# The MLP of a two-layer decoder in four parts of 16 up tiles, the up tiles of a part between the down pairs of the part before

## The chip, the core and the metric

The kernel runs on one core of a Trainium2 chip. A core has a matrix engine (TensorE, PE in the profile; its weight loads are a row of their own, PEld), a vector engine (VectorE, DVE), a scalar engine (ScalarE, ACT), GpSimd (POOL, unused here) and SyncE (SP), which here only issues DMAs. Each engine works through its own list of instructions in order and waits on semaphores. The metric is the device time of one execution in microseconds (us), lower is better.

## The reference, cut to what matters

A decoder of two layers on 256 positions of width 2048: retention, then an MLP and a gated embedding, then block attention, a second MLP and a second gated embedding. The change touches the two MLPs:

```python
def rms_norm(x, g):
    y = xf * lax.rsqrt(jnp.mean(xf * xf, axis=-1, keepdims=True) + RMS_EPS)
    return y * g
def sq_relu_mlp(xn, w_up, w_down):
    return jnp.square(jax.nn.relu(xn @ w_up)) @ w_down
...
h = h + sq_relu_mlp(rms_norm(h, mlp_norm_g[i]), mlp_w_up[i], mlp_w_down[i])
```

`w_up` is 2048 x 8192, `w_down` 8192 x 2048, all in float32.

## The kernel before

**Operands.** TensorE is fed float32r operands, and float32 accuracy is rebuilt from two of them. Each weight unit (128 x 1024 of raw float32 from a DMA) is split: ACT casts it to a high part `wh` (L254), DVE subtracts that from the raw value and leaves the low part `wl` (L255). Activations are split in the same way. A product is then three matmuls: high by high, high by low, low by high. All weights go through one stream: a ring of three raw buffers of 1 MB (`raw`, a DMA each on SP), a ring of three pairs `wh`/`wl` (`RING`), and a list `prep` of splits with a due time, counted in matmul units. `run` walks over the units: it records the splits that are due, then the unit's matmuls, then what hangs on that unit (`at`). So the order on ACT and DVE is that of due times, and how far they run ahead of PE is set by the rings.

**Up.** An up tile is 128 of the 8192 columns, kept transposed: two weight units, 32 matmuls, with the weights as the stationary operand (`phase_a`, `mm_a`, L186 and L188), into one bank of PSUM. `evac_up` takes it out: ACT copies the first half (L259), DVE adds the second (`fold`, L260), DVE squares the positive part in one instruction (L756), and `block` splits it into `a` (L609, L611).

**Down.** A pair is 256 of the 8192 rows by 1024 columns, 1 MB of weights; a `sweep` runs over pairs and adds into four banks C00, C01, C10 and C11 (two halves of positions by two of columns); `g` is the half of the 2048 output columns. An ordinary pair needs eight products of 2 x 2 blocks, three matmuls each: 24. A fast pair (`FAST`) uses a Winograd form with seven products, 21 matmuls: `sums` forms three sums of weight blocks on DVE (L731 to L733, tile `tsum`), `corner` splits the three blocks that are used as they are (1536 columns), `wide` splits the sums (2048 columns), and on the activation side `combine` forms four sums `sf` and splits them into `sh` and `sl`. Four shared banks (P1, P5, Q6, Q7) go into the results at the end of a sweep (`shared`), beside the four C banks (`collect`, L685).

**Order.** The MLP runs in two halves: 32 up tiles, then two sweeps (g = 0 and 1) of 16 pairs, of which 3, 5, 7, 9, 11 and 13 are fast; then the same again. So a layer has four sweeps with six fast pairs each.

PSUM has eight banks: four for tiles and C banks (`mm`), two `y`, two `aux`.

Of the kernel before, what the change touches and what calls it, by code (L numbers as in the profile page):

```python
# [24 lines left out]
RV = RH * RDV  # L25
AH, DH = 16, 128
GH = 4
FF = 4 * D
FH = FF // 2
PD = 256  # L30
RMS_EPS = 1e-6
GN_EPS = 1e-5
# [53 lines left out]
class Core:  # L86
# [10 lines left out]
        self.slots.append(s)  # L97
        return s

    def unit(self, src, j, mm):  # L100
# [25 lines left out]
    def narrow(self, s, u):  # L126
# [3 lines left out]
        self.split(s["h"][:, u], s["l"][:, u], raw[:, u])  # L130
        self.spent += u

    def wide(self, s, src, n):
        self.operand(s)
        h, l = (s[x].rearrange("p a b -> p (a b)")[:, :n] for x in "hl")
        self.split(h, l, src.rearrange("p a b -> p (a b)")[:, :n])

    def run(self):
        for fn in self.tasks.pop(-1, []):
# [47 lines left out]
                else:  # L187
                    mm(ps, wh[:, c], rhs[k], start=first and k == 0, stop=end)  # L188

    def phase_a(self, name, src, base, tiles, per, lead, rhs, evac):  # L190

        banks = {}
        for j, (n, u) in enumerate(order_a(tiles, per, lead)):
            def mm(wh, wl, n=n, u=u):
                if u == 0:
                    banks[n] = self.bank(f"{name}{n}", *(("y", 2) if 4 <= n < lead else ()))
                self.mm_a(banks[n], wh, wl, [rhs(u * 8 + k) for k in range(8)], u == 0, u == per - 1, u % 2 == 1)
            i = self.unit(src, base + j, mm)
# [258 lines left out]
    def retention(self):  # L457
        nc = self.nc
        mm = nc.tensor.matmul
        x, ot = {}, {}  # L460
        first = len(self.units)
# [8 lines left out]
        for hd in range(RH):  # L470
            b, st = len(self.units), {}
# [93 lines left out]
                self.at(b + 25 + c, lambda c=c, q=2 * hd + c, i=b + 25 + c, turn=turn: self.steps(i, turn(q, 2 * c)))  # L565

        for g in range(2):
            self.sweep(f"ret_out{g}_", "ret_out", g * RV // 256, RET_ORDER, RET_FAST, x, g, ((1, 2), (3, 4)) if g else ((3, 4), (5, 6)), G_MLP0)

    def add(self, gains):  # L570
        def evac(c, banks, i):
# [56 lines left out]
            x[q, name] = h[:, n * P:(n + 1) * P], l[:, n * P:(n + 1) * P]  # L628
        yield

    def sweep(self, name, src, first, order, fast, x, g, when, gain, rows=None):

        banks, left = {}, {}
        tags = {"P1": "y", "P5": "y", "Q6": "aux", "Q7": "aux"}

        def add(s, ops):
            for bank, _, _ in ops:
                left[bank] = left.get(bank, 0) + 1

            def mm():  # L640
                h, l = (s[n].rearrange("p a (b c) -> p (a b) c", b=2) for n in "hl")
                m = self.nc.tensor.matmul
                for bank, which, j in ops:
                    start = bank not in banks
                    if start:
                        banks[bank] = self.bank(f"{name}{bank}_", *((tags[bank], 2) if bank in tags else ()))
                    left[bank] -= 1
                    ps, (xh, xl) = banks[bank], x[which]
                    m(ps, xh, h[:, j], start=start, stop=False)
                    m(ps, xh, l[:, j], start=False, stop=False)  # L650
                    m(ps, xl, h[:, j], start=False, stop=left[bank] == 0)
# [83 lines left out]
    def mlp(self, layer, gains):  # L735
        nc = self.nc
        v = nc.vector
        st = {}
        b = len(self.units)

        def rows():
            st["r2"] = self.cp.tile([P, 4], F32, name="r2", tag="r2", bufs=2)
            v.tensor_mul(st["r2"][:, :2], self.rn, self.rn)
            v.tensor_scalar_mul(st["r2"][:, 2:], st["r2"][:, :2], -1.0)
        self.at(b + 4, self.stats_a)
        self.at(b + 6, rows)
        x, pair = {}, {}
        for half in range(2):
            def evac_up(n, ps, half=half):
                q = n // 2  # L750
                if n % 2 == 0:
                    pair[q] = self.slot("t", (P, 2, S))
                t = pair[q][:, n % 2]
                self.fold(t, ps)
                yield
                v.scalar_tensor_tensor(t, t, 0.0, t, op0=ALU.max, op1=ALU.mult)  # L756
                parts = []
                if n % 2:
                    z = pair.pop(q)
                    if q in FAST:  # L760
                        parts.append(self.combine(x, q, z.rearrange("p a b -> p (a b)")))
                        next(parts[0])
                yield
                yield from self.both([self.block(x, st, n, t, q in FAST and n % 2 == 0)] + parts)
            self.phase_a(f"up{half}_", f"mlp_up{layer}", half * 64, 32, 2, 1 if half else UPLEAD, lambda k: self.xx[k], evac_up)
# [361 lines left out]
```

## Time and profile before

| | |
|---|---|
| median of 3 runs | 2720.79 us (2720.36 to 2720.8) |
| the profiled execution: its own time | 2720.18 us |
| its span | 2718.4 us |
| DVE busy | 1986.8 us (73%), 2603 instructions |
| ACT busy | 1365.0 us (50%), 1790 instructions |
| PEld busy | 2300.2 us (85%) |
| read from HBM | 517.39 MB, 191 GB/s over the span |

The span goes from the first to the last instruction of the profiled execution; its own time is 1.8 us longer. A start in the timeline is us from the start of the span. A row of the timeline has the start, the duration, the engine, the line, the operation with output and inputs, and in brackets the idle time of the engine ahead of it and what ended that. The matmuls are pipelined: one shows a duration of 0.39 us, but the next starts much earlier, so that PE's progress is read from the distance of starts.

In layer 0 the MLP runs from about 740 to 1430 us, with the first sweeps from 917 and again from 1261 us; in layer 1 the same comes about 1178 us later.

### The profile page before, as it was taken

What the parts mean: (1) busy time and instruction counts of PE and PEld (TensorE: products, weight loads), DVE (VectorE), ACT (ScalarE), POOL (GpSimd) and SP (SyncE); (2) the same over time, 40 slices, a digit from 0 to 9 for tenths busy, and PEclk for the clock granted to TensorE, in tenths of its full rate; (3) what the DMA queues carried; (4) which work ended last, traced back from release to release, by engine and by line L of the source; (5) the groups of instructions that cost most, each with busy time, mean ns of one, the idle gap of its engine ahead of it and who ended that gap; (6) DMA issues with size and microseconds to landing.
All of it is one profiled execution on the core that took longest, in us unless ns stands there. A gap on an engine that the chain in (4) does not pass through costs nothing.

```text
span 2718.4 us, 33914 instructions
## 1 busy us (share of the span) xinstructions
PE 2705.2 (100%) x13564; PEld 2300.2 (85%) x13564; DVE 1986.8 (73%) x2603; ACT 1365.0 (50%) x1790; POOL 0.2 (0%) x4
## 2 busy tenths in 40 slices
PE   9999999999999999999999999999999999999998
PEld 8888888888888888888888888888888888888886
DVE  7766666678876688666896777775666887668875
ACT  6444444445544445444556555555444544445564
POOL 0000000000000000000000000000000000000000
PEclk9999999999999999999999999999999999999999
DMA  7555455545565556555564555555554655555553
GB/s 287 189 189 188 176 187 189 176 171 198 213 201 188 179 208 217 186 186 186 200 218 174 193 180 178 177 186 178 193 188 174 222 187 207 186 177 209 194 215 139
DMA packets 79449, 522.47 MB, mean 192 GB/s; under 512 B 8987, under 2 KB 12988, under 8 KB 17596
## 3 DMA queue, kind: packets, MB, share of 16 engines
q1 hardware_dynamic: 78476, 519.20, 53.3%
q8 instruction: 106, 1.74, 0.2%
q10 hardware_dynamic: 816, 1.11, 0.2%
q14 instruction: 51, 0.42, 0.0%
HBM read 517.39 MB, written 2.88 MB: 191 GB/s over the span
## 4 chain that ended last, share of the span: by engine, by line
PE 97%; DVE 2%; ACT 1%; issue 0%; DVEq 0%
PE up L188 17%; PE up L186 9%; PE qk L188 4%; PE ak L188 2%; PE qk L186 2%; PE aq L188 2%; PE ak L186 1%; PE aq L186 1%; DVE wl L255 1%; PE xt L294 1%; PE y L526 1%; PE qk L215 1%; PE pu L797 0%; DVE h L685 0%; ACT wh L254 0%
## 5 line engine op out<-in xcount | busy, mean ns | idle before, releaser
L255 DVE TENSOR_TENSOR wl<-raw,wh 128x1024 fp32r<-128x1024 f32 (+3 forms) x811 | 1113.4, 1389 | 336.9 <-ACT wh L254 335.8
L254 ACT CAST wh<-raw 128x1024 fp32r<-128x1024 f32 (+3 forms) x811 | 935.4, 1185 | 305.6 <-issue 49.6
L188 PE MATMUL up<-x,wh 128*128 128x512 f32 x2048 | 491.5, 391 | 0.0
L188 PEld LDWEIGHTS up<-x,wh 128*128 128x128 f32 x2048 | 375.7, 188 | 72.3
L186 PEld LDWEIGHTS up<-x,wl 128*128 128x128 f32 x2048 | 263.9, 191 | 11.4 <-DVE wl L255 0.6
L186 PE MATMUL up<-x,wl 128*128 128x256 f32 x2048 | 267.5, 283 | 0.0
L259 ACT COPY t<-up 128x256 f32<-128x256 f32 x128 | 47.6, 372 | 365.2 <-PE up L188 365.2
L254 ACT CAST wh<-tsum 128x2048 fp32r<-128x2048 f32 x60 | 114.8, 1914 | 197.9 <-DVE tsum L733 189.9
L255 DVE TENSOR_TENSOR wl<-tsum,wh 128x2048 fp32r<-128x2048 f32 x60 | 137.6, 2293 | 24.4 <-ACT wh L254 24.4
L260 DVE TENSOR_TENSOR t<-t,up 128x256 f32<-128x256 f32 x128 | 53.9, 421 | 115.4 <-ACT t L259 115.4
L188 PE MATMUL qk<-x,wh 128*128 128x512 f32 x448 | 110.0, 392 | 0.0
L188 PEld LDWEIGHTS qk<-x,wh 128*128 128x128 f32 x448 | 81.8, 188 | 15.6
L731 DVE TENSOR_TENSOR tsum<-raw 128x1024 f32<-128x1024 f32 x60 | 73.1, 1219 | 0.0
L188 PE MATMUL aq<-x,wh 128*128 128x512 f32 x256 | 63.2, 391 | 0.0
L188 PE MATMUL ak<-x,wh 128*128 128x512 f32 x256 | 62.9, 391 | 0.0
L186 PE MATMUL qk<-x,wl 128*128 128x256 f32 x448 | 59.8, 284 | 0.0
L186 PEld LDWEIGHTS qk<-x,wl 128*128 128x128 f32 x448 | 57.8, 191 | 2.2
L287 ACT ACTIVATE sq<-h 128x512 f32<-128x512 f32 x48 | 30.1, 629 | 57.3 <-DVE h L685 24.9
L188 PEld LDWEIGHTS ak<-x,wh 128*128 128x128 f32 x256 | 46.6, 188 | 8.8
L188 PEld LDWEIGHTS aq<-x,wh 128*128 128x128 f32 x256 | 46.5, 188 | 8.7
L756 DVE SCALAR_TENSOR_TENSOR t<-t 128x256 f32<-128x256 f32 x128 | 53.6, 419 | 0.1
L609 ACT CAST a<-t 128x256 fp32r<-128x256 f32 x104 | 42.7, 411 | 10.8 <-DVE t L756 10.8
(1272 smaller groups left out, 5276.3 us busy)
## 6 DMA issues: line engine op xcount, KB each, us to landing
raw<-mlp_up SPq DMA_DIRECT2D x128, 1024.0 KB, 4.8
raw<-mlp_dn SPq DMA_DIRECT2D x128, 1024.0 KB, 4.8
raw<-ret_in SPq DMA_DIRECT2D x94, 1024.0 KB, 4.8
raw<-att SPq DMA_DIRECT2D x48, 1024.0 KB, 4.8
raw<-ret_out SPq DMA_DIRECT2D x32, 1024.0 KB, 4.8
raw<-ple_gate SPq DMA_DIRECT2D x32, 1024.0 KB, 4.8
raw<-att_o SPq DMA_DIRECT2D x16, 1024.0 KB, 4.8
raw<-ple_up SPq DMA_DIRECT2D x4, 1024.0 KB, 4.8
```

The lines of the kernel that those rows point to most:

```text
L186: mm(ps[:, S:], wl[:, c], rhs[k][:, :S], start=False, stop=end)
L188: mm(ps, wh[:, c], rhs[k], start=first and k == 0, stop=end)
L215: m(ps, wh[:, c], x, start=u + j == 0, stop=False)
L254: self.nc.scalar.copy(dst_h, src)
L255: self.nc.vector.tensor_sub(dst_l, src, dst_h.bitcast(F32))
L259: self.nc.scalar.copy(dst, ps[:, :S])
L260: self.nc.vector.tensor_add(dst, dst, ps[:, S:])
L287: self.nc.scalar.activation(self.slot("sq"), self.h[c][:, t], AF.Square, accum_out=self.ssq[:, t, c:c + 1])
L294: self.nc.tensor.transpose(ps[:, o * P:(o + 1) * P], self.h[c][:, t, f * P:(f + 1) * P], self.ident)
L609: self.nc.scalar.copy(h, src)
L731: v.tensor_add(o[:, 0::3], r[:, 0:2], r[:, 3:4].to_broadcast([P, 2, 512]))
L756: v.scalar_tensor_tensor(t, t, 0.0, t, op0=ALU.max, op1=ALU.mult)
```

## The change

The MLP runs in four parts of 16 up tiles and 8 pairs. The 16 tiles of the first part come first, alone. Then, for parts 0, 1 and 2, each of the two sweeps of the part takes turns with up tiles of the next part: one up tile, one pair, eight times. The two sweeps of part 3 have no up tiles left and run alone. In parts 0, 1 and 2 pairs 0 to 5 of eight are fast (`MIX`), in part 3 pairs 3 and 5 (`LAST`). So a layer has eight sweeps in place of four.

Around this: in a mixed sweep the cast, the sums and the low parts of a fast pair have due times of their own (`high`, `low`, `corner(s, False)`); an up tile's two splits are both due at the first unit of the preceding pair (`ahead`); the bank C11 is of kind `y`, so that C00, C01, C10 and one up tile share the four `mm` banks; the end of the sweep (`collect`, `shared`) is spread otherwise. Relu and square of an up tile move from one DVE instruction to two on ACT. A buffer `rb` moves into the common pool, and the weights are packed in the new order on the host.

```diff
-FAST = (3, 5, 7, 9, 11, 13)
-MLP_ORDER = range(16)
+PART = 16
+MIX = (0, 1, 2, 3, 4, 5)
+LAST = (3, 5)
...
-            self.prep.append((i - (SOON if i < 12 + SOON else LOOK), lambda: self.narrow(s, j % 2)))
+            due = self.slots[-1 - ahead]["first"] if ahead else i - (SOON if i < 12 + SOON else LOOK)
+            self.prep.append((due, lambda: self.narrow(s, j % 2)))
...
+    def high(self, s, src, n):
+        self.operand(s)
+        self.nc.scalar.copy(s["h"].rearrange("p a b -> p (a b)")[:, :n], src.rearrange("p a b -> p (a b)")[:, :n])
+
+    def low(self, s, src, n):
+        h, l, w = (x.rearrange("p a b -> p (a b)")[:, :n] for x in (s["h"], s["l"], src))
+        self.nc.vector.tensor_sub(l, w, h.bitcast(F32))
+
     def wide(self, s, src, n):
-        self.operand(s)
-        h, l = (s[x].rearrange("p a b -> p (a b)")[:, :n] for x in "hl")
-        self.split(h, l, src.rearrange("p a b -> p (a b)")[:, :n])
+        self.high(s, src, n)
+        self.low(s, src, n)
...
-            a, b, due = 2 * q, 2 * q + 1, self.slots[-1 if n else -2]["first"]
-            s = self.begin(src, first + q)
+            a, b = 2 * q, 2 * q + 1
+            s = self.begin(src, first + q - base)
+            back = [z["first"] for z in self.slots[-3:-1]]
+            due = back[0] if mixed or n == 0 else back[1]
...
+                if mixed:
+                    self.prep.append((due, lambda s=s: self.high(s, self.raw(s), 3 * UC // 2)))
+                    self.prep.append((due, lambda s=s, t=t: self.sums(s, t)))
+                    self.prep.append((back[1], lambda s=s: self.corner(s, False)))
+                    self.prep.append((back[1], lambda t=t: self.wide(t, t["t"], 2 * UC)))
...
-        self.at(i - 1, lambda: self.collect(banks, g, 0, rows))
+        self.at(i if mixed else i - 1, lambda: self.collect(banks, g, 0, rows))
         self.at(i, lambda: self.collect(banks, g, 1, rows))
-        for fn, u in zip(self.shared(banks, g, rows), (e + 1, e + 2) + ((i, i) if last else (i + 1, i + 2))):
+        late = (e + 3, e + 4) if mixed else (i, i) if last else (i + 1, i + 2)
+        for fn, u in zip(self.shared(banks, g, rows), (e + 1, e + 2) + late):
...
-                v.scalar_tensor_tensor(t, t, 0.0, t, op0=ALU.max, op1=ALU.mult)
+            nc.scalar.activation(t, t, AF.Relu)
+            nc.scalar.activation(t, t, AF.Square)
...
+        self.phase_a("up0_", up, 0, PART, 2, UPLEAD, x_up, evac_up)
+        for part in range(tiles // PART):
+            last = part == tiles // PART - 1
+            b = part * PART // 2
+            for g in range(2):
+                when = (((2, 3), (5, 7)) if g else ((3, 4), (5, 6))) if last else None
+                sw = self.sweep(f"dn{part}{g}_", dn, (part * 2 + g) * PART // 2, b, range(b, b + PART // 2), fast, x, g, when, gains[0], st, not last)
+                for p in range(PART // 2):
+                    if not last:
+                        n = (part + 1) * PART + g * PART // 2 + p
+                        self.phase_a(f"up{n}_", up, 2 * n, 1, 2, 1, x_up, lambda _, ps, n=n: evac_up(n, ps), 2)
+                    next(sw)
+                next(sw, None)
```

Before, DVE's list in the middle of a down sweep of layer 0 (part of the first sweep): a fast pair, an ordinary pair, a fast pair; `tsum` are the sums of weight blocks, `wl` the low parts.

```order
L731 TENSOR_TENSOR tsum_7619<-raw_7523 128x2x512
L732 TENSOR_TENSOR tsum_7619<-tsum_7619,raw_7523 128x512
L733 TENSOR_TENSOR tsum_7619<-tsum_7619,raw_7523 128x512
L255 TENSOR_TENSOR wl_7624<-raw_7523,wh_7623 128x1536
L255 TENSOR_TENSOR wl_7654<-tsum_7619,wh_7653 128x2048
L255 TENSOR_TENSOR wl_7667<-raw_7558,wh_7666 128x2048
```

Each fast pair is followed by an ordinary one, and no up tile is near. Now, DVE's list for one turn of the first mixed sweep of layer 0: from the `fold` of up tile 17 to that of up tile 18 (`t` is an up tile in SBUF, `sf` and `sl` the activation sums of a fast block and their low part).

```order
L271 TENSOR_TENSOR t_6790<-t_6790,up17_0_6849 128x256
L266 TENSOR_TENSOR wl_6885<-raw_6747,wh_6884 128x1024 x2
L630 TENSOR_TENSOR sf_6905<-t_6790 128x256
L631 TENSOR_TENSOR sf_6905<-sf_6905,t_6790 128x128
L632 TENSOR_TENSOR sf_6905<-t_6790,sf_6905 128x128
L757 TENSOR_TENSOR tsum_6912<-raw_6800 128x2x512
L758 TENSOR_TENSOR tsum_6912<-tsum_6912,raw_6800 128x512
L759 TENSOR_TENSOR tsum_6912<-tsum_6912,raw_6800 128x512
L623 TENSOR_TENSOR a_6903<-t_6790,a_6903 128x256
L140 TENSOR_TENSOR wl_6910<-raw_6800,wh_6909 128x1536
L140 TENSOR_TENSOR wl_6936<-tsum_6912,wh_6935 128x2048
L638 TENSOR_TENSOR sl_6930<-sf_6905,sh_6929 128x512
```

The two low parts of the next up tile, the three sums, the two low parts of the next fast pair and the evacuation of the last up tile now stand in one turn; after an up tile of even number the rows `sf` and `sl` are missing and `ac`, 128 columns, stands in place of `a`. ACT's list for the same turn:

```order
L270 COPY t_6790<-up17_0_6849 128x256
L265 CAST wh_6884<-raw_6747 128x1024 x2
L784 ACTIVATE t_6790<-t_6790 128x256
L785 ACTIVATE t_6790<-t_6790 128x256
L621 CAST a_6903<-t_6790 128x256
L136 CAST wh_6909<-raw_6800 128x1536
L636 CAST sh_6929<-sf_6905 128x512
L136 CAST wh_6935<-tsum_6912 128x2048
```

The two ACTIVATE rows are relu and square, which stood on DVE; the casts of the next up tile stand ahead of them. At the end of that sweep, DVE's list from behind the last up tile's `fold` (`dn00` is this sweep, `h0` and `h1` the residual stream, `tsum_7417` the sums of the next sweep's first pair, `t_7326` up tile 23):

```order
L759 TENSOR_TENSOR tsum_7417<-tsum_7417,raw_7286 128x512
L630 TENSOR_TENSOR sf_7437<-t_7326 128x256
L631 TENSOR_TENSOR sf_7437<-sf_7437,t_7326 128x128
L632 TENSOR_TENSOR sf_7437<-t_7326,sf_7437 128x128
L709 SCALAR_TENSOR_TENSOR h0_89<-dn00_C00__6806,r2_6064,h0_89 128x512
L709 SCALAR_TENSOR_TENSOR h1_90<-dn00_C01__6802,r2_6064,h1_90 128x512
L709 SCALAR_TENSOR_TENSOR h0_89<-dn00_C10__6833,r2_6064,h0_89 128x512
L709 SCALAR_TENSOR_TENSOR h1_90<-dn00_C11__7361,r2_6064,h1_90 128x512
L623 TENSOR_TENSOR a_7435<-t_7326,a_7435 128x256
L140 TENSOR_TENSOR wl_7415<-raw_7286,wh_7414 128x1536
L140 TENSOR_TENSOR wl_7465<-tsum_7417,wh_7464 128x2048
L638 TENSOR_TENSOR sl_7459<-sf_7437,sh_7458 128x512
```

The four `collect` rows stand behind the sums and ahead of the low parts of the next sweep's first pair.

More of the change, by code (lines that the diff above doesn't have):

```diff
@@ L28 @@
 FF = 4 * D
-FH = FF // 2
 PD = 256
@@ L98, in begin, with unit @@
         return s
-    def unit(self, src, j, mm):
+    def unit(self, src, j, mm, ahead=None):
         i = len(self.units)
@@ L131, in narrow, with raw @@
         self.spent += u
+    def high(self, s, src, n):
[4 more added lines that the diff above has]
+        self.nc.vector.tensor_sub(l, w, h.bitcast(F32))
     def wide(self, s, src, n):
-        self.operand(s)
-        h, l = (s[x].rearrange("p a b -> p (a b)")[:, :n] for x in "hl")
-        self.split(h, l, src.rearrange("p a b -> p (a b)")[:, :n])
+        self.high(s, src, n)
+        self.low(s, src, n)
+    def raw(self, s):
+        return self.pairs[s["pair"]]["raw"]
     def run(self):
@@ L188, in mm_a, with phase_a @@
                     mm(ps, wh[:, c], rhs[k], start=first and k == 0, stop=end)
-    def phase_a(self, name, src, base, tiles, per, lead, rhs, evac):
+    def phase_a(self, name, src, base, tiles, per, lead, rhs, evac, ahead=None):
         banks = {}
@@ L197, in mm @@
                 self.mm_a(banks[n], wh, wl, [rhs(u * 8 + k) for k in range(8)], u == 0, u == per - 1, u % 2 == 1)
-            i = self.unit(src, base + j, mm)
+            i = self.unit(src, base + j, mm, ahead)
             if u == per - 1:
@@ L356, in spread @@
             self.nc.tensor.matmul(ps[:, t * P:(t + 1) * P], r[:, t:t + 1].to_broadcast([P, P]), self.ident, start=True, stop=True)
-        rb = self.cp.tile([P, S], F32, name="rb", tag="rb", bufs=1)
+        rb = self.slot("rb", (P, S))
         self.nc.scalar.copy(rb, ps[:, :S])
@@ L567, in retention @@
         for g in range(2):
-            self.sweep(f"ret_out{g}_", "ret_out", g * RV // 256, RET_ORDER, RET_FAST, x, g, ((1, 2), (3, 4)) if g else ((3, 4), (5, 6)), G_MLP0)
+            for _ in self.sweep(f"ret_out{g}_", "ret_out", g * RV // 256, 0, RET_ORDER, RET_FAST, x, g, ((1, 2), (3, 4)) if g else ((3, 4), (5, 6)), G_MLP0):
+                pass
     def add(self, gains):
@@ L629, in combine, with sweep @@
         yield
-    def sweep(self, name, src, first, order, fast, x, g, when, gain, rows=None):
+    def sweep(self, name, src, first, base, order, fast, x, g, when, gain, rows=None, mixed=False):
         banks, left = {}, {}
         tags = {"P1": "y", "P5": "y", "Q6": "aux", "Q7": "aux"}
+        if mixed:
+            tags["C11"] = "y"
         def add(s, ops):
@@ L721, in whole, with corner @@
         self.spent += 1
-    def corner(self, s):
-        self.wide(s, self.pairs[s["pair"]]["raw"], 3 * UC // 2)
+    def corner(self, s, both=True):
+        if both:
+            self.high(s, self.raw(s), 3 * UC // 2)
+        self.low(s, self.raw(s), 3 * UC // 2)
         self.spent += 1
@@ L747, in mlp @@
         x, pair = {}, {}
[L748 to L765, printed above, removed]
-            for g in range(2):
-                when = (((2, 3), (5, 7)) if g else ((3, 4), (5, 6))) if half else None
-                self.sweep(f"dn{half}{g}_", f"mlp_dn{layer}", (half * 2 + g) * FH // 256, MLP_ORDER, FAST, x, g, when, gains[0], st)
+        tiles, blocks = FF // P, FF // 256
@@ new lines, in mlp, with evac_up @@
+        fast = [q for q in range(blocks) if q % (PART // 2) in (MIX if q < blocks - PART // 2 else LAST)]
+        def evac_up(n, ps):
+            q = n // 2
+            if n % 2 == 0:
+                pair[q] = self.slot("t", (P, 2, S))
+            t = pair[q][:, n % 2]
+            self.fold(t, ps)
+            yield
+            nc.scalar.activation(t, t, AF.Relu)
+            nc.scalar.activation(t, t, AF.Square)
+            gens = [self.block(x, st, n, t, q in fast and n % 2 == 0)]
+            if n % 2:
+                z = pair.pop(q)
+                if q in fast:
+                    gens.append(self.combine(x, q, z.rearrange("p a b -> p (a b)")))
+            yield from self.both(gens)
@@ new lines, in mlp, with x_up @@
+        up, dn = f"mlp_up{layer}", f"mlp_dn{layer}"
+        def x_up(k):
+            return self.xx[k]
+        self.phase_a("up0_", up, 0, PART, 2, UPLEAD, x_up, evac_up)
+        for part in range(tiles // PART):
+            last = part == tiles // PART - 1
+            b = part * PART // 2
+            for g in range(2):
+                when = (((2, 3), (5, 7)) if g else ((3, 4), (5, 6))) if last else None
[6 more added lines that the diff above has]
+                next(sw, None)
@@ L1106 @@
         up, dn = arr(mlp_w_up)[i], arr(mlp_w_down)[i]
-        data[f"mlp_up{i}"] = pack(np.concatenate([cut_a(up[:, :FH], UPLEAD), cut_a(up[:, FH:], 1)]))
-        parts = [cut_s(dn[:FH, :1024]), cut_s(dn[:FH, 1024:]), cut_s(dn[FH:, :1024]), cut_s(dn[FH:, 1024:])]
+        data[f"mlp_up{i}"] = pack(np.concatenate([cut_a(up[:, :PART * P], UPLEAD), cut_a(up[:, PART * P:], 1)]))
+        parts = [cut_s(dn[k:k + PART * P, c:c + 1024]) for k in range(0, FF, PART * P) for c in (0, 1024)]
         data[f"mlp_dn{i}"] = pack(np.concatenate(parts))
```

9 lines of the change are left out of this document (6 added, 3 removed).

## The prediction

> **What bounds the kernel now.** I read the page first, then PE's timeline in both kinds of stage, then what DVE does there.
>
> ```profile
> span 2718.4 us, 33914 instructions
> PE 2705.2 (100%) x13564; PEld 2300.2 (85%) x13564; DVE 1986.8 (73%) x2603; ACT 1365.0 (50%) x1790; POOL 0.2 (0%) x4
> PE 97%; DVE 2%; ACT 1%; issue 0%; DVEq 0%
> ```
>
> TensorE is busy all the time, and the chain of waits lies on it for 97%. A busy PE need not be a PE without gaps, so the distances between starts decide. The table of windows for a stretch of down sweeps and one of up tiles (PEclk 1.00 is the full granted clock):
>
> ```profile
> core 0: us, PE busy (x) PEld busy (x) DVE busy (x) ACT busy (x) POOL busy (x), PEclk, DMA share, GB/s
> 925.00:1085.00 160.00, 160.00 (x707) 132.49 (x706) 137.85 (x104) 79.70 (x49) 0.00 (x0) 1.00 0.59 209
> 1085.00:1260.00 175.00, 175.00 (x1012) 154.81 (x1011) 117.73 (x181) 80.51 (x127) 0.00 (x0) 1.00 0.54 191
> ```
>
> PE's timeline: three pieces of up tiles; the first matmul of a fast pair and of the pair behind it; two rows of ordinary pairs, 45 matmuls apart; and the last matmul of a sweep with the first of the up tile behind it:
>
> ```profile
> 1164.90 3.82 PE L188 MATMUL up<-x,wh 128*128 128x512 f32 x16
> 1168.55 2.08 PE L186 MATMUL up<-x,wl 128*128 128x256 f32 x16
> 1170.46 3.82 PE L188 MATMUL up<-x,wh 128*128 128x512 f32 x16
> ...
> 933.64 0.39 PE L649 MATMUL dn_C__7494<-wh,sh 128*128 128x512 f32 x1
> 938.40 0.39 PE L649 MATMUL dn_C__7487<-wh,a 128*128 128x512 f32 x1
> ...
> 990.08 0.39 PE L649 MATMUL dn_C__7487<-wh,a 128*128 128x512 f32 x1
> 1000.28 0.39 PE L649 MATMUL dn_C__8021<-wh,a 128*128 128x512 f32 x1
> ...
> 1083.01 0.39 PE L651 MATMUL dn_C__8044<-wh,a 128*128 128x512 f32 x1
> 1083.24 1.98 PE L188 MATMUL up<-x,wh 128*128 128x512 f32 x8
> ```
>
> A matmul of a sweep takes (1000.28 - 990.08) / 45 = 0.2267 us of PE. A fast pair takes 938.40 - 933.64 = 4.76 us, which is 21 of these; an ordinary one 24, 5.44 us; an up tile 1170.46 - 1164.90 = 5.57 us. The 707 matmuls in 160 us of sweeps are 160.3 us by this distance: no gaps. So PE's work is the time, and what the change takes from PE counts in full as long as the other engines deliver.
>
> **The change, part by part.**
>
> *PE.* A layer had 4 sweeps of 6 fast pairs, 24; it gets 6 of 6 and 2 of 2, 40. That is 32 more fast pairs in two layers, each 24 - 21 = 3 matmuls shorter: 96 matmuls, which is the difference of the two PE lists. 96 x 0.2267 = **21.8 us less**. No other matmul of PE's is added or removed, and a switch between pair and up tile is free: 1083.01 to 1083.24 is the usual distance.
>
> *DVE.* Each fast pair costs DVE three sums and a low part more than an ordinary one, and what were two stages with DVE busy for 137.85 of 160 us (86%) and 117.73 of 175 (67%) become one, in turns. A turn (up tile and fast pair) is 5.57 + 4.76 = 10.33 us of PE. What it costs DVE I take from starts, since neighbours overlap by some 0.08 us:
>
> ```profile
> 935.83 2.29 DVE L255 TENSOR_TENSOR wl<-raw,wh 128x2048 fp32r<-128x2048 f32 x1 [1.32 <-ACT wh L254]
> 938.03 1.22 DVE L731 TENSOR_TENSOR tsum<-raw 128x1024 f32<-128x1024 f32 x1
> 939.29 0.69 DVE L732 TENSOR_TENSOR tsum<-tsum,raw 128x512 f32<-128x512 f32 x1
> 940.02 0.69 DVE L733 TENSOR_TENSOR tsum<-tsum,raw 128x512 f32<-128x512 f32 x1
> 940.63 1.75 DVE L255 TENSOR_TENSOR wl<-raw,wh 128x1536 fp32r<-128x1536 f32 x1
> 942.77 2.29 DVE L255 TENSOR_TENSOR wl<-tsum,wh 128x2048 fp32r<-128x2048 f32 x1 [0.39 <-ACT wh L254]
> ...
> 940.82 1.91 ACT L254 CAST wh<-tsum 128x2048 fp32r<-128x2048 f32 x1 [3.46 <-DVE tsum L733]
> ...
> 1174.06 1.23 DVE L255 TENSOR_TENSOR wl<-raw,wh 128x1024 fp32r<-128x1024 f32 x1 [0.73 <-ACT wh L254]
> 1175.20 0.42 DVE L756 SCALAR_TENSOR_TENSOR t<-t 128x256 f32<-128x256 f32 x1
> 1175.65 0.42 DVE L618 TENSOR_TENSOR sf<-t 128x256 f32<-128x256 f32 x1
> 1176.11 0.29 DVE L619 TENSOR_TENSOR sf<-sf,t 128x128 f32<-128x128 f32 x1
> 1176.44 0.29 DVE L620 TENSOR_TENSOR sf<-t,sf 128x128 f32<-128x128 f32 x1
> 1176.65 0.28 DVE L611 TENSOR_TENSOR ac<-t,ac 128x128 fp32r<-128x128 f32 x1
> 1176.85 1.22 DVE L255 TENSOR_TENSOR wl<-raw,wh 128x1024 fp32r<-128x1024 f32 x1
> L626 DVE TENSOR_TENSOR sl<-sf,sh 128x512 fp32r<-128x512 f32 x30 | 20.6, 685 | 0.0
> ```
>
> From start to start: up low part 1.14, 2048-column low part 2.20, the sums 1.26 + 0.73 + 0.61, `sf` 0.46 + 0.33 + 0.21, `ac` 0.20; by the same overlap `fold` and `a` 0.34, `sl` 0.60. The low part of the sums waits for ACT's cast: the third sum ends at 940.71, the cast runs from 940.82, the low part starts at 942.77, 2.06 later, and the 1536-column part and `a` or `ac` fit in between. So a turn without `sf`: 0.34 + 2 x 1.14 + 1.26 + 0.73 + 0.69 + 2.06 + 2.20 = 9.56; one with `sf` and `sl` adds 1.00 + 0.60: 11.16. They alternate; the mean is **10.36 us of DVE against 10.33 of PE**. This is the point on which the forecast stands.
>
> *Slack.* The rest of what stands on DVE in a mixed sweep, and ACT beside an up tile's end:
>
> ```profile
> L685 DVE SCALAR_TENSOR_TENSOR h<-q,r,h 128x512 f32<-128x512 f32 x24 | 18.0, 750 | 0.6
> 1003.34 0.68 DVE L711 TENSOR_TENSOR q<-q,dn_Q__7615 128x512 f32<-128x512 f32 x1
> ...
> 1166.94 0.37 ACT L259 COPY t<-up 128x256 f32<-128x256 f32 x1 [2.99 <-PE up L188]
> 1167.20 0.41 ACT L609 CAST a<-t 128x256 fp32r<-128x256 f32 x1
> 1167.51 2.00 ACT L254 CAST wh<-raw 128x1024 fp32r<-128x1024 f32 x2
> ```
>
> Count from the end of an up tile on PE. The low part of the sums must be there one pair, one up tile and ten matmuls later: 10.33 + 2.27 = 12.6. ACT copies the tile from 0.23 on (1166.94; the tile's eight last matmuls, from 1164.90, end at 1166.71), then casts for the next up tile from 0.5 to 1.55 and 2.55. So DVE cannot start those low parts before 1.6; in a turn with `sf` the `fold` stands in effect at 1.26, the low part of the sums starts 0.34 + 2.28 + 1.00 + 1.26 + 0.73 + 0.69 + 2.06 = 8.36 later and ends at 1.26 + 8.36 + 2.29 = 11.9. The slack is 0.7 us, and five more turns at 0.03 use 0.15 of it: PE does not wait in the six fast turns. From tile 21 to tile 24 lie two ordinary pairs and the sweep's end: on DVE three `fold`, six up low parts, two ordinary low parts, one set of sums with its two low parts, two `sf` and `sl`, three `a` or `ac`, eight additions at 0.75 and four at 0.69, together 1.0 + 6.8 + 4.4 + 2.6 + 3.9 + 3.2 + 0.9 + 6.0 + 2.8 = 31.6 us, beside 4.76 + 3 x 5.57 + 2 x 5.44 = 32.3 of PE. There the lag does not grow. For a mean turn of c us the loss over the 12 mixed sweeps is 12 x max(0, 5 x (c - 10.33) - 0.7): **0 at 10.36**.
>
> *ACT.* Relu and square are not in the trace. The nearest rows are the copy above, 0.37, and an ACTIVATE with a scale:
>
> ```profile
> L277 ACT ACTIVATE x<-xt,g 128x256 fp32r<-128x256 f32 x48 | 20.3, 479 | 15.3 <-PE xt L294 15.3
> raw<-mlp_dn SPq DMA_DIRECT2D x128, 1024.0 KB, 4.8
> ```
>
> I take 0.40 each, near the copy, since neither reads a scale; the ends are 0.37 and 0.48. They run behind the casts, from 2.55 to 3.4 (at most 3.6), while `sf` is not reached before 3.9. ACT is busy for 79.70 of 160 us in sweeps, so 0.8 more in a turn of 10.33 has room. They cost nothing, and take 0.42 us off DVE's turn. What they were later than 3.9 would add to the turns with `sf`.
>
> [...]
>
> *DMA.* A turn needs 2 MB in 10.33 us, 203 GB/s; the sweeps of before already moved 209. An up tile's raw buffer is free at 3.9, the pair that takes it is cast in the next turn, some 10 us on, and landing takes 4.8 (the row above): nothing. *Banks.* An up tile has one `mm` bank left; its `fold` ends by 2.6, and the next tile starts at 4.76: nothing. If DVE were 2 us later, PE would wait here too. *Ring.* The cast of the sums takes the `wh` that the pair before frees at 4.76, and its sums are ready at 6.6 at the earliest: nothing. *Ends.* Up to the first sweep and from the last fast pair on (an ordinary, a fast and two ordinary pairs) the order is as before: nothing.
>
> **Sum.** Against the profiled execution 2720.18 - 21.8 = 2698.4; the median of the runs is 0.6 higher than that execution, so **2699.0 us**. A change under 0.2% (5.4 us) can't be told from none.
>
> **Rivals.**
> *DVE a little late* (chance 0.17). If neighbours on DVE do not overlap in this mix, each costs its full duration: 0.42 + 2.45 + 1.22 + 0.69 + 0.69 + 0.28 + 1.75 + 2.29 = 9.8 without `sf`, 11.6 with it, c = 10.72, the loss 12 x (5 x 0.39 - 0.7) = 15 us: 2714. For it speaks the thin margin; against it, that all rows above overlap. [...]
> *DVE becomes the bound: slower* (0.07). Full durations, and ahead of each low part of the sums the 0.39 us of waiting that the row at 942.77 shows, because ACT's cast comes as late as there: c = 11.11, the loss 12 x (5 x 0.78 - 0.7) = 38 us: 2737. It is slower from c = 10.83 on, where the loss reaches 21.8. Against it: between the sums and that low part there is now `a` or `ac`, which fills the 0.39.
> *The change does not reach PE* (0.02): the lists differ by 96 matmuls, so only a wrong distance of starts could do it: 2720.
> *Lower than the sum* (0.02): PE has no gaps to win, 2697 at the least.
>
> **How the numbers follow.** The forecast, PE without gaps, has 0.72. The range takes in c up to 10.69, a loss of 13 us, and two us below: 2697 to 2713, with some 0.84 of the chance; beyond lie the slower case and the last third of the late one. Faster by over 0.2% holds for c under 10.74: 0.86, the forecast and most of the late case; within it 0.07; slower 0.07.
>
> **What would show it.** PE: 21 matmuls at 0.2267 and a turn of 10.33 us; a longer turn, with PE or PEld waiting for `wl<-tsum`, is the late rival. DVE: 1.6 us from an up tile's end to its low parts in turns with `sf` and DVE hardly idle in mixed stretches. ACT: two ACTIVATE rows of about 0.40, behind the casts. If PE waits first at the start of a sweep, my account of the ordinary turns is wrong; if for `wh`, that of ACT.

## The result, and the profile after

| | before | after |
|---|---|---|
| median (4 runs each) | 2720.57 us (2720.34 to 2720.8) | 2699.03 us (2698.78 to 2699.29) |
| the profiled execution: its own time | 2720.18 us | 2698.78 us |

The ratio is 0.9921, 95% interval 0.9904 to 0.9938: 21.5 us less. The page of the changed kernel, the lines on span, engines and chain:

```profile
span 2697.0 us, 34064 instructions
PE 2683.3 (99%) x13468; PEld 2281.7 (85%) x13468; DVE 2151.0 (80%) x2763; ACT 1523.5 (56%) x2102; POOL 0.2 (0%) x4
PE 97%; DVE 2%; ACT 1%; issue 0%; DMA 0%; SPq 0%; DVEq 0%
```

The span is 21.4 us shorter, PE busy 21.9 us less with 96 matmuls fewer, while DVE gained 164 us of work and ACT 159 us: none of that reached the end. The windows of the first and of the second mixed sweep, each from its second fast pair over its two ordinary pairs and its end to behind the first fast pair of the next sweep:

```profile
core 0: us, PE busy (x) PEld busy (x) DVE busy (x) ACT busy (x) POOL busy (x), PEclk, DMA share, GB/s
844.00:924.00 80.00, 80.00 (x406) 68.43 (x406) 77.06 (x90) 51.30 (x66) 0.00 (x0) 1.00 0.57 199
924.00:1013.00 89.00, 89.00 (x461) 76.48 (x461) 83.09 (x88) 54.54 (x68) 0.00 (x0) 1.00 0.58 204
```

PE is busy all the time, but DVE is now busy for 77.06 of 80 us. Busy time does not show gaps, so the starts decide again: in both layers all turns with a fast pair take 10.33 us and all with an ordinary pair 11.01 (5.57 + 5.44), over the sweeps' ends too. One turn on PE, the first matmuls of up tile, fast pair and up tile, from its timeline:

```profile
859.59 1.98 PE L199 MATMUL up<-x,wh 128*128 128x512 f32 x8
865.16 0.39 PE L663 MATMUL dn_C__6802<-wh,sh 128*128 128x512 f32 x1
869.92 1.98 PE L199 MATMUL up<-x,wh 128*128 128x512 f32 x8
875.48 0.39 PE L663 MATMUL dn_C__6802<-wh,sh 128*128 128x512 f32 x1
```

5.57 us and 4.76 us, 10.33 together, as in the two stages of before. DVE's timeline over two turns, one without `sf` and one with it, from `fold` (L271) to `fold`:

```profile
856.84 0.41 DVE L271 TENSOR_TENSOR t<-t,up 128x256 f32<-128x256 f32 x1
...
861.42 0.69 DVE L759 TENSOR_TENSOR tsum<-tsum,raw 128x512 f32<-128x512 f32 x1
862.03 0.28 DVE L623 TENSOR_TENSOR ac<-t,ac 128x128 fp32r<-128x128 f32 x1
862.23 1.75 DVE L140 TENSOR_TENSOR wl<-raw,wh 128x1536 fp32r<-128x1536 f32 x1
864.15 2.29 DVE L140 TENSOR_TENSOR wl<-tsum,wh 128x2048 fp32r<-128x2048 f32 x1 [0.16 <-ACT wh L136]
866.36 0.41 DVE L271 TENSOR_TENSOR t<-t,up 128x256 f32<-128x256 f32 x1
866.71 2.36 DVE L266 TENSOR_TENSOR wl<-raw,wh 128x1024 fp32r<-128x1024 f32 x2
868.99 0.42 DVE L630 TENSOR_TENSOR sf<-t 128x256 f32<-128x256 f32 x1
...
874.69 2.29 DVE L140 TENSOR_TENSOR wl<-tsum,wh 128x2048 fp32r<-128x2048 f32 x1
876.90 0.69 DVE L638 TENSOR_TENSOR sl<-sf,sh 128x512 fp32r<-128x512 f32 x1
877.50 0.41 DVE L271 TENSOR_TENSOR t<-t,up 128x256 f32<-128x256 f32 x1
```

The turns take 866.36 - 856.84 = 9.52 us and 877.50 - 866.36 = 11.14 us, mean 10.33. The low part of the sums ends at 874.69 + 2.29 = 876.98; PE wants it ten matmuls into the pair that begins at 875.48, at 877.75. So 0.77 us of slack is left. That the mean is PE's 10.33 to the digit is no measure of DVE's own need: in every second turn DVE's low parts for the next up tile (the row at 866.71) start right behind ACT's first cast, which ends at 866.67 and waits in its turn for the end of the tile on PE, at 865.16. DVE is held to PE there; the rows show that it keeps up, not how far below 10.33 it could go. In the first four mixed sweeps of each layer the slack is 0.77 and 0.98 us by turns from the third to the sixth fast turn; it does not shrink. In the last two it is mostly 1.76, as `sf` and `sl` are formed for only two of their sixteen up tiles in place of six (part 3 has two fast pairs). ACT in the second of the turns above:

```profile
865.36 0.37 ACT L270 COPY t<-up 128x256 f32<-128x256 f32 x1 [1.24 <-PE up L199]
865.62 2.01 ACT L265 CAST wh<-raw 128x1024 fp32r<-128x1024 f32 x2
867.52 0.42 ACT L784 ACTIVATE t<-t 128x256 f32<-128x256 f32 x1
867.97 0.42 ACT L785 ACTIVATE t<-t 128x256 f32<-128x256 f32 x1
```

The square ends at 868.39, and DVE comes to `sf` at 868.99.

### The profile page after: what moved, and what is told of

Its sections match the earlier page's. It is cut to its first block, busy times and chain, and to the rows that moved or that the text cites. A ratio compares the mean times of both kernels' runs of the same rounds, so it can differ in the third digit from the quotient of the medians.

```text
span 2697.0 us, 34064 instructions
## 1 busy us (share of the span) xinstructions
PE 2683.3 (99%) x13468; PEld 2281.7 (85%) x13468; DVE 2151.0 (80%) x2763; ACT 1523.5 (56%) x2102; POOL 0.2 (0%) x4
## 4 chain that ended last, share of the span: by engine, by line
PE 97%; DVE 2%; ACT 1%; issue 0%; DMA 0%; SPq 0%; DVEq 0%
PE up L199 17%; PE up L197 9%; PE qk L199 4%; PE ak L199 2%; PE qk L197 2%; PE aq L199 2%; PE ak L197 1%; PE aq L197 1%; PE xt L305 1%; PE y L537 1%; DVE wl L266 0%; PE pu L837 0%; PE qk L226 0%; DVE h L709 0%; DMA raw<-ret_in 0%
## 5 line engine op out<-in xcount | busy, mean ns | idle before, releaser
L266 DVE TENSOR_TENSOR wl<-raw,wh 128x1024 fp32r<-128x1024 f32 (+1 forms) x651 | 772.1, 1216 | 180.6 <-ACT wh L265 179.6
L265 ACT CAST wh<-raw 128x1024 fp32r<-128x1024 f32 (+1 forms) x651 | 656.7, 1046 | 191.1 <-issue 49.9
L199 PE MATMUL up<-x,wh 128*128 128x512 f32 x2048 | 506.4, 391 | 0.0
L140 DVE TENSOR_TENSOR wl<-raw,wh 128x1536 fp32r<-128x1536 f32 (+1 forms) x160 | 316.0, 1980 | 43.2 <-ACT wh L136 42.7
L136 ACT CAST wh<-raw 128x1536 fp32r<-128x1536 f32 (+1 forms) x160 | 266.0, 1665 | 56.5 <-PE dn_C__20877 L665 11.4
L136 ACT CAST wh<-tsum 128x2048 fp32r<-128x2048 f32 x92 | 176.1, 1914 | 185.3 <-DVE tsum L759 162.6
L140 DVE TENSOR_TENSOR wl<-tsum,wh 128x2048 fp32r<-128x2048 f32 x92 | 210.8, 2291 | 19.1 <-ACT wh L136 17.9
L757 DVE TENSOR_TENSOR tsum<-raw 128x1024 f32<-128x1024 f32 x92 | 112.0, 1218 | 0.0
L271 DVE TENSOR_TENSOR t<-t,up 128x256 f32<-128x256 f32 x128 | 53.4, 417 | 41.8 <-ACT t L270 39.3
L759 DVE TENSOR_TENSOR tsum<-tsum,raw 128x512 f32<-128x512 f32 x92 | 63.7, 692 | 3.1
L758 DVE TENSOR_TENSOR tsum<-tsum,raw 128x512 f32<-128x512 f32 x92 | 63.7, 692 | 3.1
```

What stands on the lines that cost most here:

```text
L136: self.nc.scalar.copy(s["h"].rearrange("p a b -> p (a b)")[:, :n], src.rearrange("p a b -> p (a b)")[:, :n])
L140: self.nc.vector.tensor_sub(l, w, h.bitcast(F32))
L265: self.nc.scalar.copy(dst_h, src)
L266: self.nc.vector.tensor_sub(dst_l, src, dst_h.bitcast(F32))
L271: self.nc.vector.tensor_add(dst, dst, ps[:, S:])
L757: v.tensor_add(o[:, 0::3], r[:, 0:2], r[:, 3:4].to_broadcast([P, 2, 512]))
```

## The experiments

All are edits of the changed kernel. "Before" is timed anew on the same chip each time: 2721.58, 2720.91, 2721.19 and 2721.08 us for the four groups below. The changed kernel is not; as before's median moves by up to 1.0 us from group to group, differences to 2699.03 of that size say nothing by themselves, and for these the turns on PE in the traces decide. My theory: PE's work is the time, and DVE's turn stays under it by a thin margin. The first rival is that PE's waits would have been hidden or made up in any case, so that DVE's margin decides nothing; the second that the gain comes from taking turns and not from the fewer matmuls.

### The margin: a little more work on DVE and on ACT

**Square on DVE** (as before the change):

```diff
-            nc.scalar.activation(t, t, AF.Relu)
-            nc.scalar.activation(t, t, AF.Square)
+            v.scalar_tensor_tensor(t, t, 0.0, t, op0=ALU.max, op1=ALU.mult)
```

> The squaring goes back from two ACT instructions to one DVE instruction; all else as in the changed kernel. Theory (DVE's turn sets a limit, the lag starts anew in each sweep): the DVE turn grows by 0.34 to 0.45 us, mean 0.40, and the loss is 12 x (5 x 0.40 - 0.75) = 15 us: 2714 us (2711 to 2717), with PE waiting for the low part of the sums in the later fast turns of each mixed sweep. Rival 1, DVE has more room than counted: 2699. Rival 2, no recovery in the ordinary turns, the lag adds up over 72 turns: 72 x 0.40 less one start, 2727.

Measured: 2712.48 us (2712.27 to 2712.68), ratio 0.9967, interval 0.9955 to 0.9979: 13.5 us of the gain are gone. DVE's `fold`, the square and the next `fold` in a turn without `sf`, then the starts of three up tiles on PE:

```profile
879.28 0.41 DVE L271 TENSOR_TENSOR t<-t,up 128x256 f32<-128x256 f32 x1
881.89 0.42 DVE L784 SCALAR_TENSOR_TENSOR t<-t 128x256 f32<-128x256 f32 x1
889.16 0.41 DVE L271 TENSOR_TENSOR t<-t,up 128x256 f32<-128x256 f32 x1
```

```profile
870.47 1.98 PE L199 MATMUL up<-x,wh 128*128 128x512 f32 x8
881.45 1.98 PE L199 MATMUL up<-x,wh 128*128 128x512 f32 x8
891.97 1.98 PE L199 MATMUL up<-x,wh 128*128 128x512 f32 x8
```

DVE's short turn grew from 9.52 to 9.88, and PE's turns are now 10.98 and 10.52 us in place of 10.33. So 0.4 us on DVE in each turn is enough to make PE wait. The size came out as the formula gave it, but in part by luck. In this trace only eight of the twelve mixed sweeps lose time: 0.9 us in each with g = 0, 2.2 to 2.6 in each with g = 1, whose first turns are late already; the four sweeps of part 2, with few `sf`, lose almost nothing. The formula had 1.2 for each of twelve. The view of waits lists none of these waits, as it leaves out short ones (2.6 us for PE in all, 2.4 in the changed kernel); the distances of starts show them.

**Low part of `ac` twice**, and **low parts of `a` and `ac` twice**: one more subtraction into the same tile, first 128 columns in every second turn, then in every turn.

```diff
-        self.nc.vector.tensor_sub(l, src, h.bitcast(F32))
+        for _ in range(2 if half and "r2" in st else 1):
+            self.nc.vector.tensor_sub(l, src, h.bitcast(F32))
```

(The second has no `half` in the condition.)

> A low part of 128 columns (ac) is computed twice, in every second turn: 0.20 us of DVE more, 0.10 in the mean turn. Theory (a threshold): 5 x 0.10 = 0.5 is below the slack of 0.75 us that the trace shows, so nothing: 2699 (up to 2700). Rival, every added DVE microsecond counts: 72 x 0.10 = 7 us: 2706.

> All low parts of the MLP's activations (a and ac) are computed twice: 0.20 and 0.34 us more, 0.27 in the mean turn. Theory (threshold, then five turns of a sweep): 12 x (5 x 0.27 - 0.75) = 7 us: 2706 (2704 to 2710). Rival 1, no limit on DVE: 2699. Rival 2, every turn pays: 72 x 0.27 = 19 us: 2718.

Measured: 2699.34 us (2698.96 to 2699.62) and 2700.74 us (2700.42 to 2701.24). The first is nothing, as expected, and its turns on PE stay at 10.33 us; the second cost 1.7 us and not 7. DVE's timeline of the second in a turn without `sf`:

```profile
857.24 0.41 DVE L271 TENSOR_TENSOR t<-t,up 128x256 f32<-128x256 f32 x1
...
862.43 0.61 DVE L624 TENSOR_TENSOR ac<-t,ac 128x128 fp32r<-128x128 f32 x2
862.96 1.75 DVE L140 TENSOR_TENSOR wl<-raw,wh 128x1536 fp32r<-128x1536 f32 x1
864.63 2.28 DVE L140 TENSOR_TENSOR wl<-tsum,wh 128x2048 fp32r<-128x2048 f32 x1
866.83 0.41 DVE L271 TENSOR_TENSOR t<-t,up 128x256 f32<-128x256 f32 x1
```

The turn is 9.59 us, only 0.07 longer: the added work stands between the sums and their low part, and there DVE waited 0.16 us for ACT's cast before (the row at 864.15 above). The turn with `sf` is 878.27 - 866.83 = 11.44 by the same view, 0.30 longer. The mean grows by 0.19, and 12 x (5 x 0.19 - 0.77) = 2.2 us is near the measured 1.7. What failed in the expectation was mainly the size of the added work. The formula, again, counts twelve sweeps: in the trace eight lose, 0.14 us each with g = 0 and 0.28 with g = 1, together 1.7, and those of part 2 nothing.

**Relu twice on ACT:**

```diff
             nc.scalar.activation(t, t, AF.Relu)
+            nc.scalar.activation(t, t, AF.Relu)
```

> Relu runs twice on ACT (the second changes nothing): 0.45 us more of ACT in each turn, nothing on DVE. Theory (ACT has room: the square ends some 0.6 us before DVE reaches sf): 2699, at most 2700. Rival (ACT is as near to its limit as DVE): 72 x 0.45 = 32 us less a start, 2722 to 2731.

Measured: 2699.68 us (2698.82 to 2700.07). 0.45 us more on ACT in every turn costs nothing that can be told apart, and the turns on PE stay at 10.33; the room of 0.6 us ahead of `sf` takes it.

### What makes the gain

**Four of eight pairs fast in the mixed sweeps:**

```diff
-MIX = (0, 1, 2, 3, 4, 5)
+MIX = (0, 1, 2, 3)
```

> Mixed sweeps with four fast pairs of eight in place of six; part 3 as it is. 12 sweeps x 2 pairs x 3 = 72 matmuls more. Theory (PE without gaps on both sides, time follows the count of matmuls): 2699.0 + 72 x 0.2267 = 2715.3 (2714.5 to 2716). Rival (the changed kernel hides some waiting on DVE in its fast turns, or the turns gain by themselves): less than 16 us more.

Measured: 2715.75 us (2714.79 to 2716.08), ratio 0.9981, interval 0.9971 to 0.999. 72 matmuls more cost 16.7 us, 0.232 each, close to PE's distance of 0.2267. Against before this run has 24 matmuls fewer, 5.4 us, and is 5.2 us faster: nothing is left for the turns themselves.

**The same fast pairs, not in turns:** the 16 up tiles of a part ahead of its two sweeps.

```diff
+            if part:
+                self.phase_a(f"up{part}_", up, 2 * part * PART, PART, 2, 1, x_up, lambda n, ps, part=part: evac_up(part * PART + n, ps))
...
-                sw = self.sweep(..., st, not last)
-                for p in range(PART // 2):
...
-                    next(sw)
-                next(sw, None)
+                for _ in self.sweep(..., st):
+                    pass
```

> Same parts, same fast pairs, but the 16 up tiles of a part come ahead of its two sweeps instead of between the pairs of the part before, with the due times of the unmixed sweep. Theory (the turns are what lets DVE keep up): a fast pair costs DVE 1.26 + 0.73 + 0.69 + 2.06 + 2.20 = 6.9 us against 4.76 of PE, so two sweeps of a part lack 12 x 6.9 + 4 x 2.2 + 17.6 - (12 x 4.76 + 4 x 5.44) = 30 us, less some 9 that fall beside up tiles: 6 x 22 to 6 x 30, 2830 to 2880. Rival (the products alone give the gain): 2699.

Measured: 2879.67 us (2879.08 to 2880.54), ratio 1.0584, interval 1.0568 to 1.06, at the upper edge. PE's waits in the trace: what waits for what, us in total, times, longest:

```profile
PE dn_P__7063 L663 <- DVE q L739: 7.3, 1, 7.3
PE dn_C__6745 L664 <- DVE wl L140: 6.8, 5, 1.4
```

In one sweep five matmuls into one bank wait for low parts, and the next sweep's first P bank waits for the additions at the end of the one before. Over the whole trace the view gives 82.8 us of waiting for low parts and 36.5 us for such additions, and the granted clock is 0.50 for 61 us. The run goes back to the unmixed sweep in its due times, its bank for C11 and its sweep's end as well, so that the price is that of the whole arrangement and not of the order alone. With this said, neither half of the change does it alone: the fast pairs take the matmuls away, and the up tiles between them give DVE the time to follow.

**The low part of the sums behind the next `fold`:** only the cast keeps its due time.

```diff
-                    self.prep.append((back[1], lambda t=t: self.wide(t, t["t"], 2 * UC)))
+                    self.prep.append((back[1], lambda t=t: self.high(t, t["t"], 2 * UC)))
+                    self.prep.append((s["first"], lambda t=t: self.low(t, t["t"], 2 * UC)))
```

> Only the due time of the sums' low part is changed, to the pair's own first unit: on DVE it then stands behind the fold of the up tile, which waits for the end of that tile on PE. Theory (DVE's in-order list sets PE's wait): fold 0.6 to 0.95 after the tile's end, low part until 3.25, wanted at 2.27: PE waits 1.0 us in each of 72 fast turns: 2771 (2762 to 2778), with PE waiting for the low part of tsum. Rival (only the sum of DVE's work counts, not its order): 2699.

Measured: 2782.72 us (2782.27 to 2782.99), ratio 1.0227, interval 1.0212 to 1.0243. The mechanism is as expected, at 84 us in place of 72. PE's timeline around the wait:

```profile
859.58 0.39 PE L663 MATMUL dn_P__6825<-wh,sh 128*128 128x512 f32 x1
860.82 0.50 PE L664 MATMUL dn_P__6825<-wl,sh 128*128 128x512 f32 x1 [0.86 <-DVE wl L140]
861.16 0.39 PE L665 MATMUL dn_P__6825<-wh,sl 128*128 128x512 f32 x1
```

The matmul that needs the low part starts 1.24 us after the one ahead, 1.01 more than the usual 0.2267: that is the wait I had expected. But the one behind it comes after 0.34 us, 0.11 too late as well. In this trace up tiles start at 857.54 and 869.02, a turn of 11.48, 1.15 longer; 72 x 1.15 = 83 us. So each of these waits costs PE a little more than its length; the matmul behind the late one comes 0.34 us after it in all 72 fast turns.

### Where the gain ends

**Seven of eight fast:**

```diff
-MIX = (0, 1, 2, 3, 4, 5)
+MIX = (0, 1, 2, 3, 4, 5, 6)
```

> Mixed sweeps with seven fast pairs of eight: 12 x 3 = 36 matmuls fewer, 8.2 us of PE. Theory: DVE per mixed sweep 7 x 10.36 + 14.2 = 86.7 us against 83.3 of PE; with one ordinary turn there is no recovery, so 3.4 x 12 = 41 us of waiting: 2699 - 8 + 41 = 2732 (2722 to 2738). Rival (DVE has more room than counted): 2691.

Measured: 2728.83 us (2727.89 to 2730.04), ratio 1.003, interval 1.0019 to 1.0041. 36 matmuls fewer on PE (8.2 us), and yet 29.8 us more than with six. PE's timeline at the start of the second sweep, then PE's windows there and at the start of a later sweep, and two windows of 3.41 us that the text below needs:

```profile
917.37 0.39 PE L663 MATMUL dn_C__7526<-wh,sh 128*128 128x512 f32 x1
920.53 0.79 PE L664 MATMUL dn_C__7526<-wl,sh 128*128 128x512 f32 x1 [2.77 <-DVE wl L140]
921.12 0.63 PE L665 MATMUL dn_C__7526<-wh,sl 128*128 128x512 f32 x1
921.55 0.63 PE L663 MATMUL dn_C__7530<-wh,a 128*128 128x512 f32 x1
```

```profile
core 0: us, PE busy (x), PEclk, DMA share, GB/s
920.00:926.40 6.40, 5.87 (x14) 0.50 0.46 166
1095.40:1101.00 5.60, 5.52 (x24) 1.00 0.52 187
916.38:919.79 3.41, 1.38 (x7) 1.00 0.00 0
1093.87:1097.28 3.41, 1.80 (x8) 1.00 0.22 41
```

With one ordinary pair left, DVE does not catch up before the sweep's end, where the additions stand ahead of the next low part; PE waits 2.77 us for it. Here the granted clock then falls to 0.50 and matmuls come every 0.43 us up to 926.4; behind a wait of the same length at 1095 it stays at 1.00. By the starts on PE, the first turn of each sweep that follows a mixed sweep's end, ten in both layers, takes 12.8 to 16.2 us in place of 10.33, and the other turns are as long as before. The excess of the ten is 38.9 us, all of the 38 between 2690.8 and 2728.8: the waiting matmuls start 2.1 to 2.9 us late, 27 us in all, matmuls at half the clock cost some 9 us, and the late second matmuls 2. So the expectation came near for a part of its reason only: it had 41 us of waiting for DVE, in twelve sweeps, and nothing for the clock.

The trace also shows when the clock falls. The five stretches at 0.50 begin at 919.79, 1182.62, 2189.55, 2363.63 and 2452.37 us; each lasts 3.41 us (the first twice that), and the distances between them are 77, 295, 51 and 26 times 3.413 us. So in this trace they lie on a fixed grid, and what sets the waits apart is how much of one falls into one window of it. In the windows ahead of the two stretches in layer 0 PE was idle for 2.03 us (1.38 us busy in the one that ends at 919.79, above) and for 2.40 us (the wait ahead of the matmul at 1181.67). Windows with 1.61 us of idle time (the wait at 1095, split over two windows, 1.80 us busy in the second) and with 1.75 us (the part after 1267.92, 102 windows behind 919.79, of the 2.77 us ahead of the matmul at 1269.67) were followed by the full clock. Why the first stretch lasts for two windows stays open. In the run with `LAST = (3, 4, 5)`, below, 1.87 us of waiting, from 1399.52 to 1401.39, were followed by 0.50 for 3.4 us; what lies between 1.75 and 1.87 us is not shown.

**Two of the three sums on GpSimd**, with six and with seven of eight:

```diff
-        v.tensor_add(o[:, 1], o[:, 0], r[:, 1])
-        v.tensor_add(o[:, 2], o[:, 1], r[:, 2])
+        self.nc.gpsimd.tensor_add(o[:, 1], o[:, 0], r[:, 1])
+        self.nc.gpsimd.tensor_add(o[:, 2], o[:, 1], r[:, 2])
```

> The changed kernel with the second and third of the three sums of a fast pair (512 columns each) on GpSimd in place of VectorE. My theory: VectorE's turn becomes shorter by 0.73 + 0.61 = 1.34 us, mean about 9.0, but TensorE has no gap to win, so 2699.0 us (2698.5 to 2700) as long as the two sums on GpSimd, p each, are ready when ScalarE casts them: about 2.1 us lie between the end of VectorE's first sum and the latest start of that cast, so p up to about 1.05 us. Rival A: GpSimd is slower than that; then TensorE waits in most of the 72 fast turns: at p = 1.5 that is up to 72 x 0.9 = 65 us, 2764. Rival B: TensorE is not gapless and a quicker VectorE gains: under 2696.

> Seven of eight pairs fast in the mixed sweeps, and the second and third sum on GpSimd. If what limited seven of eight was VectorE's time alone, and GpSimd's two sums come in time, its 36 fewer matmuls count in full: 2699.0 - 36 x 0.2267 = 2690.8 us (2690 to 2693). Rival A: GpSimd's sums come late, then it is above 2699, by as much as in the run with six of eight and more. Rival B: seven of eight was limited by the order at the sweep's end (additions ahead of the next low parts), not by VectorE's total; then it stays near 2720.

Measured: 2873.06 us (2872.48 to 2875.29), ratio 1.056, interval 1.0544 to 1.0575, and 2937.87 us (2937.45 to 2939.07), ratio 1.0798. The first is far above all that I had allowed; the second is above 2699 by more than the first, as its rival A had it. GpSimd's and DVE's timelines of the first:

```profile
857.88 2.89 POOL L758 TENSOR_TENSOR tsum<-tsum,raw 128x512 f32<-128x512 f32 x1 [11.03 <-ACT wh L136]
860.84 1.29 POOL L759 TENSOR_TENSOR tsum<-tsum,raw 128x512 f32<-128x512 f32 x1
871.26 1.35 POOL L758 TENSOR_TENSOR tsum<-tsum,raw 128x512 f32<-128x512 f32 x1 [9.12 <-DVE tsum L757]
872.69 2.68 POOL L759 TENSOR_TENSOR tsum<-tsum,raw 128x512 f32<-128x512 f32 x1
```

```profile
857.86 1.75 DVE L140 TENSOR_TENSOR wl<-raw,wh 128x1536 fp32r<-128x1536 f32 x1
...
871.38 2.85 DVE L140 TENSOR_TENSOR wl<-raw,wh 128x1536 fp32r<-128x1536 f32 x1
```

A sum alone takes 1.3 us on GpSimd. Beside DVE's low part, whichever starts second is lengthened by nearly what the first still has to run: the sum at 857.88, just behind the low part of 857.86, takes 2.89 in place of 1.29; the low part at 871.38, behind the sum of 871.26, takes 2.85 in place of 1.75; the sum at 872.69 runs until 1.14 us after that low part ends. In these rows two engines that I counted as side by side work one after the other. Whether DVE's time is what limits seven of eight, this pair of runs therefore did not tell.

**Three of eight in the unmixed sweeps:** `LAST = (3, 4, 5)` and `LAST = (3, 5, 6)` in place of `(3, 5)`.

> LAST = (3, 4, 5): three fast pairs of eight in the two unmixed sweeps of each MLP in place of two, 4 more in all, 12 matmuls fewer: 2699.0 - 12 x 0.2267 = 2696.3 us if VectorE keeps up, and again only PE's work counts (2696 to 2697). There VectorE needs 1.26 + 0.73 + 0.61 + 1.67 + 0.47 + 2.20 = 6.9 us for a fast pair against 4.76 of PE, so three in a row put it 2 x 2.2 = 4.4 us behind; it waits 3.1 us for ScalarE's casts ahead of them, which is slack that PE does not see. Rival: the slack is not enough or the casts themselves come late, and PE waits up to 2 us in each of the four sweeps: 2699 to 2705.

> LAST = (3, 5, 6): the same 12 matmuls fewer, with one pair of fast neighbours (5 and 6) in place of three in a row: VectorE falls 2.2 us behind once. My theory: 2696.3 us (2696 to 2697). Rival: the shared banks of pair 6 are released nearer to the sweep's end, and the next sweep or the next stage waits for them: 2698 to 2702.

Measured: 2710.6 us (2710.43 to 2711.6) and 2716.4 us (2715.26 to 2717.81): slower than the changed kernel by 11.6 and 17.4 us, and beyond the rivals' prices too. DVE's timeline of the first in layer 0:

```profile
1345.75 2.29 DVE L140 TENSOR_TENSOR wl<-tsum,wh 128x2048 fp32r<-128x2048 f32 x1 [3.12 <-ACT wh L136]
1348.08 1.22 DVE L757 TENSOR_TENSOR tsum<-raw 128x1024 f32<-128x1024 f32 x1
...
1353.23 2.29 DVE L140 TENSOR_TENSOR wl<-tsum,wh 128x2048 fp32r<-128x2048 f32 x1 [0.71 <-ACT wh L136]
1355.56 1.22 DVE L757 TENSOR_TENSOR tsum<-raw 128x1024 f32<-128x1024 f32 x1
```

The 3.12 us that I had taken for slack is still there: DVE waits for a cast while the work of the following pairs stands behind it in its list, and cannot be drawn forward. The next fast pair then takes 1355.56 - 1348.08 = 7.48 us of DVE, not 6.9, beside 4.76 of PE. PE's waits, by the view of waits, grow from 2.4 us in the changed kernel to 12.0 here and to 15.1 with `(3, 5, 6)`, where 6.2 of them stand in the stage behind the MLP. With the 2.7 us of matmuls saved there are 14.3 and 20.1 us to explain; beside these 9.6 and 12.7 stand waits too short for the view and, once in each trace, a granted clock of 0.50, for 3.4 and for 6.8 us. No run came out under the changed kernel.

## Why the prediction was right

**PE's term** held: 21.8 us forecast, 21.5 measured, 21.9 in PE's busy time. That it is the matmuls, each at its distance, and not the turns, is shown by four of eight: 72 given back cost 16.7 us.

**DVE's turn** held to 0.04 us: 9.52 and 11.14 measured, 9.56 and 11.16 forecast. The mean is PE's 10.33 and not 10.36: DVE keeps up, and is held to PE in every second turn; the 0.15 us that five turns were to take off the slack is not in the trace. Neighbours on DVE overlap in this mix too: the low part at 864.15 and the `fold` at 866.36 are 2.21 us apart at a duration of 2.29. That takes away the late rival's premise, which rested on full durations. The slack was 0.77 us for 0.7. One step was too coarse: the forecast gave all twelve mixed sweeps the same mean turn, but the four of part 2 have few `sf` and `sl`, and their slack is mostly 1.76. For the changed kernel this made no difference, as the loss was 0 either way.

**The loss beyond the slack** was only an argument when I wrote it. With the squaring on DVE it cost 13.5 us where the formula, at 0.34 us more in each turn and so 10.70 in the mean, gives 12 x (5 x 0.37 - 0.7) = 14; with the small additions 0 and 1.7. The thin margin was real; the agreement of 13.5 with 14 is in part luck, as eight sweeps paid it, by 0.9 to 2.6 us, and not twelve by 1.2. The move of relu and square to ACT is worth 13.5 of the 21.5 us, so that leaving them on DVE would have been the costlier choice here.

**ACT** took 0.42 us for each of the two new instructions, between the 0.37 and 0.48 that I had as ends; they finish 0.6 us ahead of `sf`, and one more of them cost nothing.

**The sweep's end** held: no row of a mixed sweep in PE's waits of the changed kernel, and no turn on PE longer than 10.33 and 11.01 us. The slower rival, DVE as the bound, is not wrong as a mechanism: it begins one fast pair further on, and first at the place that the balance of 31.6 against 32.3 us had named as close, the start of the next sweep.

**DMA, banks and ring** at nothing are borne out only by the absence of waits; no run varied them alone.

## What to carry to other kernels

When PE is without gaps, each matmul removed counts at its distance (0.2267 us here), but only while every engine that feeds it stays under PE's time in the same stretch: work out the turn of each engine from starts, not from shares of busy time, and put work beside work that leaves that engine idle. A wait in a list is slack only if what stands behind it can be moved ahead of it. Once the margin was used up here, the price was paid in the later turns of a stretch, and each wait of PE cost some 0.1 us on top (0.34 us to the next matmul in place of 0.23). Where only some stretches are tight, count those alone.

## What the hardware showed that I had not expected

- A wait cost PE more than its length: the matmul behind the one that waited came 0.34 us after it, not 0.23.
- Whether the clock falls is not set by the length of a wait alone: after 2.77 us of waiting the granted clock was 0.50 for about 6 us in one case and 1.00 in another. In the run with seven of eight the low stretches lie on a grid of 3.413 us; a window with PE idle for 2.03 us was followed by 0.50, one with 1.75 us was not.
- A 512-column sum on GpSimd (1.3 us) and a low part on DVE (1.75 us) ran one after the other: 2.9 us for the one that started second.
- Small work added on DVE ahead of a wait of 0.16 us filled the wait: of two subtractions of 0.28 us the second lengthened its turn by 0.07.
